# Two transformer blocks on one core: a norm's factors on the weights' rows instead of on the transposed tokens

## The chip, the cores and the metric

One core of one Trainium2 chip runs the whole kernel. The metric is device time in microseconds of one execution. Below, PE is TensorE, DVE is VectorE, ACT is ScalarE, POOL is GpSimd and SP is SyncE; "PEld" is PE's loading of a stationary operand.

## What is computed

The input is 256 tokens of width 1024. A first block of two hybrid layers (retention, sparse attention, a linear recurrence, each ending in a layer norm) is followed by a second block of two layers, all in float32. The second block is where the change is:

```python
def rmsnorm(x, g):
    y = xf * lax.rsqrt(jnp.mean(xf * xf, axis=-1, keepdims=True) + EPS)
    return y * g

def second_block(x, ...):
    h = x
    for i in range(2):
        u = rmsnorm(h, norm_mix[i])
        if i == 0:
            h = h + dsw_mixer(u, a_w_qkv, ...)     # dilated sliding windows
        else:
            h = h + moba_mixer(u, b_w_qkv, ...)    # block attention
        h = h + sq_relu_mlp(rmsnorm(h, norm_ffn[i]), ffn_w1[i], ffn_w2[i])
    return h
```

Each of the four norms has two factors: one per token (the reciprocal root, which the kernel applies after the matrix products) and one per column of the 1024 (`g`, four vectors in all). A product `(x * g) @ W` is the same as `x @ (g[:, None] * W)`, so `g` can go to the tokens or to the rows of the weights.

## The kernel before

Every matrix product in float32 is made of three products of halves. A tensor is split into a high part, rounded to the type float32r, and a low part, the remainder; then `high*high + high*low + low*high` is summed in PSUM (`mm3`, L314 to L316; L415 and L416 in `b_wide`, which makes two of the three in one instruction of 512 columns). The split is one ACT instruction (a copy into float32r, L324) and one DVE instruction (source minus high part, L325), in `split`.

**Weights** lie in DRAM already packed in the order of use, in chunks of two halves. `load_half` gives a half two buffers `wh` and `wl` (eight of each, `W_BUFS`) and a raw buffer `wr` (three, `R_BUFS`), issues one DMA on SP and splits the whole half with one ACT and one DVE instruction. So the raw buffer of the third half back must have been read by DVE before the next DMA is issued, and the `wh` buffer of the eighth half back must have been let go by PE before ACT can write. A half holds 128 rows of the weights in each of several "row blocks" k laid side by side: two blocks of 384 columns for the dilated-window projections (`dq`, `dk`, `dv`; 48 halves), two of 512 for the block-attention projections (`mqk` 16 halves, `mv` 8), four of 256 for the up-projections (`f1`, 64 halves over both layers). Output and down-projections (`do`, `mo`, `f2`) follow no norm.

**Tokens** are kept both plain (`xn`, two tiles of 128 tokens) and transposed and split (`xh`, `xl`: 8 row blocks by 256 tokens). After each sublayer the steps `R{t}.{hf}` (tile t, column half hf) add the sublayer's output to `xn` on DVE (L944, L946; in the hybrid layer the layer norm of L833 and L834) and call `transposed`: four PE transposes into one PSUM bank (L863), then the split into `x`. Where a norm follows, `transposed` multiplies the four row blocks by their factors while it splits them: four ACT instructions with `scale=g[j]` (L870) and four DVE instructions (L872), each 128 columns. Where none follows (between the two hybrid layers, `gi is None`), it calls `split`, one ACT and one DVE instruction of 512 columns. There are four such norms and four calls per norm. The factors lie in `par`, one value per partition, loaded at the start.

**Order of work.** Within a sublayer the steps are issued in an order written by hand in a string (`HYB`, `DSW`, `MOBA`, `FFN`), then the framework orders each engine's queue by simulated times; steps in brackets keep their written order on PE. The end of the second hybrid layer is `... S1 ] R0.0 [ R0.1 R1.1 ] R1.0`: the second tile's upper columns come before its lower ones. The dilated-window stage starts `k0.0 b1 q0.0 k0.1 q0.1 k1.0 v0.0 k1.1 q1.0 q1.1 v0.1 v1.0 ...`, where `k1.0` loads the weights of k1 (four halves) and projects tile 0, and `k1.1` projects tile 1 with the same weights. After a projection of q or k, `head_norm` copies it on ACT (L904), squares it, sums on DVE (L907), takes a power on POOL (L426), scales on DVE, and PE transposes it (L991); the result is split for the scores (L501 and L503 for keys). The feed-forward stage runs `U{c}` (up-projection of chunk c: weights `f1`, product in `b_wide`, L1112 to L1114 and a split of the result) and `D{c}.{t}` (down-projection, weights `f2`); `U{c+3}` is issued behind `D{c}`, and the first chunk (`E`) runs by tiles, so that it can start on tile 0.

The functions that the change touches, as they were:

Of the kernel before, what the change touches and what calls it, by code (L numbers as in the profile page):

```python
# [9 lines left out]
F32 = mybir.dt.float32  # L10
F32R = mybir.dt.float32r
AF = mybir.ActivationFunctionType
OP = mybir.AluOpType
# [62 lines left out]
    return out  # L76


CHUNKS = _chunks()
OFFS, _o = {}, 0  # L80
for _k, (_a, _l, _r, _c) in CHUNKS.items():
# [8 lines left out]
P_POS, P_CW, P_CB, P_BA, P_BX, P_LAM, P_GAIN, P_G = 0, 128, 144, 148, 152, 156, 160, 164  # L90
# [181 lines left out]
def body(ctx, tc, a, out, stop=None):  # L272
    nc = tc.nc
    V, A, T, G = nc.vector, nc.scalar, nc.tensor, nc.gpsimd
    wts = a["wts"]
# [18 lines left out]
    def load_half(key, i, pieces=1):  # L294
        off, nk, n = OFFS[key]
        m = nk // 2 * n
        h = wp.tile([128, 1024], F32R, name="wh", tag="wh", bufs=W_BUFS)
        l = wp.tile([128, 1024], F32R, name="wl", tag="wl", bufs=W_BUFS)
        rt = wp.tile([128, 1024], F32, name="wr", tag="wr", bufs=R_BUFS)
        w = m // pieces  # L300
        for c in range(0, m, w):
            raw = rt[:, c:c + w]
            nc.sync.dma_start(raw, bass.AP(tensor=wts.tensor, offset=wts.offset + off + i * 128 * m + c,
                                           ap=[[m, 128], [1, w]]))
            split(h[:, c:c + w], l[:, c:c + w], raw)
        return h, l
# [15 lines left out]
    def split(h, l, src):  # L322

        A.activation(h, src, AF.Copy)  # L324
        V.tensor_tensor(l, src, h.bitcast(F32), op=OP.subtract)  # L325


    zero = cst.tile([128, 128], mybir.dt.bfloat16, name="zero")
# [177 lines left out]
    kz = [one.tile([128, 2, 2, S], F32R, name=n, tag=n, bufs=1) for n in ("kh", "kl")]  # L506


    def hybrid(l, nxt, before):
        nonlocal xh, xl, xb  # L510
        ys = [new_y() for _ in range(4)]
        qkT = one.tile([128, 4, S], F32, name="qkT", tag="qkT", bufs=1)
# [316 lines left out]
        def norm(t, hf):  # L829

            q = halves[hf]
            nm, rs, sub = mem["norm", t]
            V.scalar_tensor_tensor(xn[t][:, q], xn[t][:, q], nm, gb[0][:, q], op0=sub, op1=OP.mult)  # L833
            V.scalar_tensor_tensor(xn[t][:, q], xn[t][:, q], rs, gb[1][:, q], op0=OP.mult, op1=OP.add)  # L834
            transposed(xT, t, hf, nxt)

        halves = [slice(hf * 512, hf * 512 + 512) for hf in range(2)]
        gb, xT = [], []
# [16 lines left out]
        run(steps, HYB[l])  # L855
        xh, xl, xb = xT

    def transposed(xT, t, hf, gi):

        tp = bank("s", "xtp")  # L860
        for j in range(4):
            c = hf * 512 + j * 128
            T.transpose(tp[:, j * 128:j * 128 + 128], xn[t][:, c:c + 128], ident)  # L863
        h, l = (x[:, 4 * hf:4 * hf + 4, t * 128:t * 128 + 128] for x in xT[:2])
        tv = tp.rearrange("p (j s) -> p j s", j=4)
        if gi is None:
            return split(h, l, tv)
        g = [par[:, P_G + 8 * gi + 4 * hf + j:P_G + 8 * gi + 4 * hf + j + 1] for j in range(4)]
        for j in range(4):
            A.activation(h[:, j], tv[:, j], AF.Copy, scale=g[j])  # L870
        for j in range(4):
            V.scalar_tensor_tensor(l[:, j], tv[:, j], g[j], h[:, j].bitcast(F32), op0=OP.mult, op1=OP.subtract)  # L872

    def rms(name):

# [15 lines left out]
    def new_keys(shape):  # L891

        return [pool.tile(shape, F32R, name=n, tag=n, bufs=2) for n in ("akh", "akl")]

    def scaled_split(h, l, src, g):

        A.activation(h, src, AF.Copy, scale=g)
        V.scalar_tensor_tensor(l, src, g, h.bitcast(F32), op0=OP.mult, op1=OP.subtract)

    def head_norm(src, n, r, r2, name):  # L900

# [30 lines left out]
                             start=i == 0, stop=i == n - 1)  # L932
        return op[:, :256]

    def residual_steps(os_, scale, gi):

        xT = []

        def add(t, hf):
            if gi is not None and not xT:  # L940
                xT.extend(new_xT())
            q = slice(hf * 512, hf * 512 + 512)
            if scale is None:
                V.tensor_tensor(xn[t][:, q], xn[t][:, q], os_[t][hf], op=OP.add)  # L944
            else:
                V.scalar_tensor_tensor(xn[t][:, q], os_[t][hf], scale[t], xn[t][:, q], op0=OP.mult, op1=OP.add)  # L946
            if gi is not None:
                transposed(xT, t, hf, gi)
            else:
                nc.sync.dma_start(out[t * 128:t * 128 + 128, q], xn[t][:, q])  # L950
        return xT, {f"R{t}.{hf}": (lambda t=t, hf=hf: add(t, hf)) for t in range(2) for hf in range(2)}

    def dsw(r, gi):


        nonlocal xh, xl, xb
# [67 lines left out]
        for s in range(4):  # L1024
            steps |= {f"b{s}": lambda s=s: biased(s), f"w{s}": lambda s=s: weighted(s)}
            for t in range(2):
                steps |= {f"{n}{s}.{t}": lambda n=n, s=s, t=t: proj(n, s, t) for n in "qkv"}
                steps[f"a{s}.{t}"] = lambda s=s, t=t: attend(s, t)
        xT, more = residual_steps(os_, None, gi)
        run(steps | more, DSW)  # L1030
        if xT:
            xh, xl, xb = xT

    def moba(r, gi):
        nonlocal xh, xl, xb
        r2 = squares(r, "r2")
        ys = [new_y() for _ in range(4)]
        mem = {}

        def biased(s):  # L1040
            mem["b", s] = bias = pool.tile([128, 4, 256], F32, name="mbias", tag="bias", bufs=2)
            nc.sync.dma_start(bias, a["mb"][s].rearrange("p (n w) -> p n w", w=256))

        def proj(s, t):
            if t == 0:
                mem["w", s] = [load(("mqk", s, j)) for j in (0, 1)]
                mem["q", s] = new_q()
                mem["k", s] = new_keys([128, 2, 2, S])
            o = bank("acc", "mqk")
            a_proj(mem["w", s], o, t)  # L1050
            x = head_norm(o, 8, r[t], r2[t], "m")
            tp = bank("t", "mtp")
            for j in range(4):
                T.transpose(tp[:, j * 128:j * 128 + 128], x[:, j * 128:j * 128 + 128], ident)
            tv = tp.rearrange("p (j s) -> p j s", j=4)
            q = slice(t * 128, t * 128 + 128)
            scaled_split(*(x[:, :2, q] for x in mem["q", s]), tv[:, 0:2], gains[:, 1:2])
            halves_split(*([x[:, :, hd, q] for hd in range(2)] for x in mem["k", s]), tv[:, 2:4])

        def mv(s):  # L1060
            v = mem["v", s] = pool.tile([128, 2, 512], F32, name="mv", tag="v", bufs=V_BUFS)
            c = [load(("mv", s, j)) for j in (0, 1)]
            for t in range(2):
                o = bank("acc", "mv")
                a_proj(c, o, t)
                A.activation(v[:, t], o, AF.Copy, scale=r[t])

        def attend(s, p, t):
            bias, (qh, ql), k, v = (mem[x, s // 2 * 2 if x == "v" else s] for x in "bqkv")
            n = 128 * (t + 1)  # L1070
            c = 256 * (s % 2) + 128 * p
            q = slice(t * 128, t * 128 + 128)
            sc = bank("s", "as")
            mm3(sc[:, :2 * n].rearrange("p (h n) -> p h n", h=2), qh[:, p, q], ql[:, p, q],
                *(x[:, p, :, :n] for x in k), True, True)
            pt = softmax_unit([[(sc[:, n * hd:n * hd + n], bias[:, 2 * p + hd, 256 - n:])] for hd in range(2)], n)
            mem["pt", s, p, t] = [[(v[:, j, c + 64 * hd:c + 64 * hd + 64],
                                    pt[:, hd * n + j * 128:hd * n + j * 128 + 128]) for j in range(t + 1)]
                                  for hd in range(2)]

        def weighted(s, p):
            op = values([mem.pop(("pt", s, p, t)) for t in range(2)])
            split(ys[s][0][:, p], ys[s][1][:, p], op)
        os_, steps = out_steps([("mo", j) for j in range(4)], ys)
        for s in range(4):
            steps[f"b{s}"] = lambda s=s: biased(s)
            if s % 2 == 0:
                steps[f"v{s}"] = lambda s=s: mv(s)
            for t in range(2):
                steps[f"q{s}.{t}"] = lambda s=s, t=t: proj(s, t)  # L1090
                for p in range(2):
                    steps[f"a{s}.{p}.{t}"] = lambda s=s, p=p, t=t: attend(s, p, t)
                    steps[f"w{s}.{p}"] = lambda s=s, p=p: weighted(s, p)
        xT, more = residual_steps(os_, None, gi)
        run(steps | more, MOBA)
        if xT:
            xh, xl, xb = xT

    def ffn(i, gi):
        nonlocal xh, xl, xb  # L1100
        os_ = accumulators()
        hid, w2 = {}, {}
# [49 lines left out]
                V.tensor_tensor(q, x, x, op=OP.mult)  # L1152
                r2.append(q)
        r2 = []
        xT, steps = residual_steps(os_, r2, gi)
        steps |= {"E": lambda: up_early(EARLY), "r": norms}
        steps |= {f"U{c}": lambda c=c: up(c) for c in range(16) if c not in EARLY}
        steps |= {f"D{c}.{t}": lambda c=c, t=t: down_step(c, t) for c in range(16) for t in range(2)}
# [10 lines left out]
            behind(xn[t], src)  # L1169
            nc.sync.dma_start(xn[t], a["xn"][t])  # L1170

    hybrid(0, None, load_x)
    if stop == 1:
        return dump()
    hybrid(1, 0, None)
    if stop == 2:
        return dump()
    ctx1.close()
    pool = ctx.enter_context(tc.tile_pool(name="block2", bufs=1, reuse_waits="tile"))
    dsw(rms("r"), 1 if stop != 3 else None)  # L1180
    if stop == 3:
        return
    ffn(0, 2 if stop != 4 else None)
    if stop == 4:
        return
    moba(rms("r"), 3 if stop != 5 else None)
    if stop == 5:
        return
    ffn(1, None)


def build(arrays, stop=None):
# [19 lines left out]
```

## Time and profile before

| | us |
|---|---|
| runs | 929.26, 930.4, 933.69 (median 930.4) |
| the profiled execution, its own time | 932.65 |
| its span, first to last instruction | 930.9 |
| PE busy | 906.0 (97%) |
| PE loading weights | 786.3 (84%) |
| DVE busy | 659.3 (71%) |
| ACT busy | 533.9 (57%) |
| DMA | 155.22 MB, mean 167 GB/s |

The stages by time: the first hybrid layer to about 154 us, the second to 305, dilated windows to 450, the first feed-forward stage to 629, block attention to 747, the second feed-forward stage to the end. A matmul's busy time covers its pipelined end, so that PE's 97% is not PE at its peak; what counts is where PE has no instruction at all. In a timeline row, the bracket at the end gives the idle time before an instruction on its engine and what ended it. In groups, "x48" is a count, and the column behind the bar is busy time and the mean of one in ns.

### The profile page before, as it was taken

What the parts mean: (1) busy time and instruction counts of PE and PEld (TensorE: products, weight loads), DVE (VectorE), ACT (ScalarE), POOL (GpSimd) and SP (SyncE); (2) the same over time, 40 slices, a digit from 0 to 9 for tenths busy, and PEclk for the clock granted to TensorE, in tenths of its full rate; (3) what the DMA queues carried; (4) which work ended last, traced back from release to release, by engine and by line L of the source; (5) the groups of instructions that cost most, each with busy time, mean ns of one, the idle gap of its engine ahead of it and who ended that gap; (6) DMA issues with size and microseconds to landing.
All of it is one profiled execution on the core that took longest, in us unless ns stands there. A gap on an engine that the chain in (4) does not pass through costs nothing.

```text
span 930.9 us, 14698 instructions
## 1 busy us (share of the span) xinstructions
PE 906.0 (97%) x5430; PEld 786.3 (84%) x5430; DVE 659.3 (71%) x1426; ACT 533.9 (57%) x1002; POOL 55.3 (6%) x59
## 2 busy tenths in 40 slices
PE   8999998999999999999999999999999999999998
PEld 6998876988978889997888888888887788888886
DVE  5778957678868788787766666658888576665662
ACT  5456852545764677776754554457777574445540
POOL 0000000000001321120000000002111000000000
PEclk9999998999999999999999999999999999999999
DMA  7765333663325446654455565655654176566551
GB/s 239 236 232 166 113 124 108 204 204 116 118 80 171 154 140 191 205 158 155 143 180 195 195 193 183 188 172 181 185 175 139 46 226 190 194 194 190 182 159 46
DMA packets 45721, 155.22 MB, mean 167 GB/s; under 512 B 5072, under 2 KB 5456, under 8 KB 45648
## 3 DMA queue, kind: packets, MB, share of 16 engines
q1 hardware_dynamic: 45648, 154.27, 52.1%
q8 instruction: 43, 0.70, 0.3%
q14 instruction: 30, 0.25, 0.1%
HBM read 153.20 MB, written 1.05 MB: 166 GB/s over the span
## 4 chain that ended last, share of the span: by engine, by line
PE 82%; DVE 8%; ACT 5%; DMA 3%; issue 1%; POOL 0%; SPq 0%; DVEq 0%; ACTq 0%
PE f L415 12%; PE o L314 8%; PE o L316 8%; PE o L315 8%; PE f L416 6%; DVE wl L325 3%; DMA wr<-in_wts 3%; PE atp L493 2%; ACT wh L324 2%; PE mqk L315 2%; PE mqk L316 2%; PE mqk L314 2%; PE aop L931 1%; PE as L314 1%; PE as L316 1%
## 5 line engine op out<-in xcount | busy, mean ns | idle before, releaser
L325 DVE TENSOR_TENSOR wl<-wr,wh 128x1024 fp32r<-128x1024 f32 (+3 forms) x285 | 327.0, 1160 | 134.7 <-ACT wh L324 132.5
L324 ACT ACTIVATE wh<-wr 128x1024 fp32r<-128x1024 f32 (+3 forms) x285 | 283.8, 1009 | 158.8 <-DMA wr<-in_wts 61.3
L415 PE MATMUL f<-x,wh 128*128 128x512 f32 x480 | 170.7, 398 | 0.0
L314 PE MATMUL o<-wh,yh 128*128 128x512 f32 x368 | 145.2, 395 | 2.3 <-ACT yh L324 1.5
L315 PE MATMUL o<-wl,yh 128*128 128x512 f32 x368 | 143.7, 391 | 0.0
L316 PE MATMUL o<-wh,yl 128*128 128x512 f32 x368 | 142.7, 392 | 0.0
L416 PE MATMUL f<-x,wl 128*128 128x256 f32 x480 | 134.9, 281 | 0.0
L415 PEld LDWEIGHTS f<-x,wh 128*128 128x128 f32 x480 | 90.2, 188 | 21.6
L416 PEld LDWEIGHTS f<-x,wl 128*128 128x128 f32 x480 | 90.6, 189 | 1.1
L314 PEld LDWEIGHTS o<-wh,yh 128*128 128x128 f32 x368 | 69.1, 188 | 18.3 <-ACT yh L324 2.4
L316 PEld LDWEIGHTS o<-wh,yl 128*128 128x128 f32 x368 | 68.9, 188 | 15.0 <-issue 0.5
L315 PEld LDWEIGHTS o<-wl,yh 128*128 128x128 f32 x368 | 69.1, 188 | 12.8
L484 ACT ACTIVATE pr<-pr,anm 128x256 f32<-128x256 f32 (+2 forms) x112 | 54.0, 486 | 7.8 <-DVE anm L481 7.6
L324 ACT ACTIVATE yh<-fz 128x512 fp32r<-128x512 f32 x30 | 19.0, 632 | 57.5 <-DVE fz L1114 57.4
L1112 ACT ACTIVATE fz<-f 128x256 f32<-128x256 f32 x60 | 22.4, 373 | 41.9 <-PE f L416 41.9
L494 ACT ACTIVATE pt<-atp 128x512 f32<-128x512 f32 (+1 forms) x56 | 31.2, 562 | 19.9 <-PE atp L493 19.6
L325 DVE TENSOR_TENSOR yl<-fz,yh 128x512 fp32r<-128x512 f32 x30 | 20.8, 692 | 19.9 <-ACT yh L324 19.9
L493 PE MATMUL atp<-ident,pr 128*128 128x128 f32 x208 | 33.5, 275 | 1.0 <-DVE akl L503 0.4
L1113 DVE TENSOR_TENSOR fz<-fz,f 128x256 f32<-128x256 f32 x60 | 25.0, 417 | 13.2 <-ACT fz L1112 13.2
L489 DVE TENSOR_SCALAR pr<-pr,adn 128x256 f32<-128x256 f32 (+2 forms) x112 | 33.0, 340 | 1.0
L493 PEld LDWEIGHTS atp<-ident,pr 128*128 128x128 f32 x208 | 25.1, 140 | 6.0 <-issue 0.7
L426 POOL TENSOR_TENSOR dms<-dms,nhalf 128x6 f32<-128x6 f32 x16 | 24.2, 1516 | 88.1 <-DVE dms L908 88.1
(311 smaller groups left out, 1849.6 us busy)
## 6 DMA issues: line engine op xcount, KB each, us to landing
wr<-in_wts SPq DMA_DIRECT2D x227, 512.0 KB, 4.1
wr<-in_wts SPq DMA_DIRECT2D x48, 384.0 KB, 3.5
bias<-in_db SPq DMA_DIRECT2D x4, 640.0 KB, 4.9
wr<-in_wts SPq DMA_DIRECT2D x8, 280.0 KB, 3.0
cw<-in_cw SPq DMA_DIRECT2D x4, 512.0 KB, 4.5
mbias<-in_mb SPq DMA_DIRECT2D x4, 512.0 KB, 3.6
xT<-in_xT SPq DMA_DIRECT2D x4, 256.0 KB, 6.5
lngb<-in_lng SPq DMA_DIRECT2D x2, 512.0 KB, 4.1
```

Of the source, the lines that this page charges most:

```text
L314: T.matmul(o, sh, mh, start=start, stop=False)
L315: T.matmul(o, sh, ml, start=False, stop=False)
L316: T.matmul(o, sl, mh, start=False, stop=stop)
L324: A.activation(h, src, AF.Copy)
L325: V.tensor_tensor(l, src, h.bitcast(F32), op=OP.subtract)
L415: T.matmul(o, c.h(k)[:, q], xb[:, k], start=k == 0, stop=False)
L416: T.matmul(o[:, 0], c.l(k)[:, q], xh[:, k], start=False, stop=k == 7)
L484: A.activation(pr[:, g], pr[:, g], AF.Exp, scale=-1.0, bias=nm[:, i:i + 1], accum_out=dn[:, i:i + 1])
L489: V.tensor_scalar(pr[:, g], pr[:, g], dn[:, i:i + 1], None, op0=OP.mult)
L493: T.transpose(tp[:, j:j + 128], pr[:, j:j + 128], ident)
L494: A.activation(pt[:, :c], tp[:, :c], AF.Copy)
L1113: V.tensor_tensor(zj, zj, o[:, 0], op=OP.add)
```

## The change

The factors leave `transposed`, which now always calls `split` on the whole 512 columns. They go into `load_half`: for a chunk whose input is normed, the half is split in one piece per row block, each by an ACT instruction with `scale` and a DVE instruction with the factor as one value per partition. The DMA of such a half is the same. `scaled_split` existed before, for the queries. The argument that named the norm (`nxt`, `gi`) becomes a flag that says whether this is the last sublayer.

```diff
+GAINS = {"dq": 0, "dk": 0, "dv": 0, "mqk": 2, "mv": 2, "f1": (1, 3)}
...
         rt = wp.tile([128, 1024], F32, name="wr", tag="wr", bufs=R_BUFS)
+        g = GAINS.get(key[0])
+        if g is not None:
+            g = P_G + 8 * (g[key[1]] if key[0] == "f1" else g)
+            nc.sync.dma_start(rt[:, :m], bass.AP(tensor=wts.tensor, offset=wts.offset + off + i * 128 * m,
+                                                 ap=[[m, 128], [1, m]]))
+            for k, row in enumerate(CHUNKS[key][2][i * nk // 2:(i + 1) * nk // 2]):
+                c = slice(k * n, k * n + n)
+                scaled_split(h[:, c], l[:, c], rt[:, c], par[:, g + row:g + row + 1])
+            return h, l
...
+    def scaled_split(h, l, src, g):
+        A.activation(h, src, AF.Copy, scale=g)
+        V.scalar_tensor_tensor(l, src, g, h.bitcast(F32), op0=OP.mult, op1=OP.subtract)
...
-    def transposed(xT, t, hf, gi):
+    def transposed(xT, t, hf):
...
-        if gi is None:
-            return split(h, l, tv)
-        g = [par[:, P_G + 8 * gi + 4 * hf + j:P_G + 8 * gi + 4 * hf + j + 1] for j in range(4)]
-        for j in range(4):
-            A.activation(h[:, j], tv[:, j], AF.Copy, scale=g[j])
-        for j in range(4):
-            V.scalar_tensor_tensor(l[:, j], tv[:, j], g[j], h[:, j].bitcast(F32), op0=OP.mult, op1=OP.subtract)
+        split(h, l, tv)
...
-    def residual_steps(os_, scale, gi):
+    def residual_steps(os_, scale, last):
...
-    dsw(rms("r"), 1 if stop != 3 else None)
+    dsw(rms("r"), stop == 3)
...
-    ffn(0, 2 if stop != 4 else None)
+    ffn(0, stop == 4)
...
-    moba(rms("r"), 3 if stop != 5 else None)
+    moba(rms("r"), stop == 5)
...
-    ffn(1, None)
+    ffn(1, True)
```

## Rows read from the trace of the kernel before

**Rows 1.** Windows by stage: length, busy time of each engine (instructions), PE clock, DMA share, GB/s

```profile
305.00:450.00 145.00, 140.91 (x908) 131.21 (x908) 115.15 (x278) 102.76 (x204) 23.70 (x16) 1.00 0.53 162
...
450.00:629.00 179.00, 178.43 (x921) 151.89 (x922) 113.95 (x151) 91.85 (x135) 1.64 (x3) 1.00 0.58 184
...
629.00:747.00 118.00, 116.83 (x633) 94.61 (x631) 91.12 (x240) 83.07 (x188) 16.45 (x9) 1.00 0.48 148
...
sum 931.00, PE 905.96 PEld 786.26 DVE 659.33 ACT 533.90 POOL 55.29; mean PE 150.99 PEld 131.04 DVE 109.89 ACT 88.98 POOL 9.22
```

**Rows 2.** Chain that ended last, shares of the span by engine

```profile
PE 82%; DVE 8%; ACT 5%; DMA 3%; issue 1%; POOL 0%; SPq 0%; DVEq 0%; ACTq 0%
```

**Rows 3.** Groups by form, the split of a weight half: busy us, mean ns, idle before, releasers

```profile
L325 DVE TENSOR_TENSOR wl<-wr,wh 128x1024 fp32r<-128x1024 f32 x227 | 274.4, 1222 | 123.2 <-ACT wh L324 121.6
...
L324 ACT ACTIVATE wh<-wr 128x1024 fp32r<-128x1024 f32 x227 | 237.0, 1058 | 128.2 <-DMA wr<-in_wts 44.8 <-PE f L415 34.0 <-PE o L316 32.6
...
L325 DVE TENSOR_TENSOR wl<-wr,wh 128x768 fp32r<-128x768 f32 x48 | 45.5, 955 | 10.3 <-ACT wh L324 9.6
...
L324 ACT ACTIVATE wh<-wr 128x768 fp32r<-128x768 f32 x48 | 40.2, 847 | 22.5 <-DMA wr<-in_wts 9.4 <-PE o L316 6.8 <-PE dk L316 2.4
```

**Rows 4.** Groups by form, the nearest rows for the new pieces and the old ones

```profile
L757 DVE SCALAR_TENSOR_TENSOR xc<-lxp,par,xc 128x256 f32<-128x256 f32 x12 | 5.3, 478 | 0.0
...
L834 DVE SCALAR_TENSOR_TENSOR xn<-xn,lrs,lngb 128x512 f32<-128x512 f32 x8 | 5.7, 745 | 0.0
...
L484 ACT ACTIVATE pr<-pr,anm 128x256 f32<-128x256 f32 x48 | 23.9, 501 | 5.8 <-DVE anm L481 5.6
...
L484 ACT ACTIVATE pr<-pr,anm 128x512 f32<-128x512 f32 x16 | 11.4, 715 | 1.8 <-DVE anm L481 1.8
...
L870 ACT ACTIVATE x<-xtp,par 128x128 fp32r<-128x128 f32 x64 | 17.9, 385 | 3.3 <-PE xtp L863 3.2
...
L872 DVE SCALAR_TENSOR_TENSOR x<-xtp,par,x 128x128 fp32r<-128x128 f32 x64 | 17.6, 342 | 1.7 <-ACT x L870 1.7
...
L494 ACT ACTIVATE pt<-atp 128x512 f32<-128x512 f32 x48 | 28.2, 594 | 17.0 <-PE atp L493 16.7
...
L944 DVE TENSOR_TENSOR xn<-xn,o 128x512 f32<-128x512 f32 x8 | 5.4, 683 | 2.0 <-PE o L316 2.0
```

**Rows 5.** Timeline: start us, us, instruction; runs of one instruction in a queue

```profile
298.53 1.41 DVE L833 SCALAR_TENSOR_TENSOR xn<-xn,lmv,lngb 128x512 f32<-128x512 f32 x2
...
303.69 2.17 ACT L870 ACTIVATE x<-xtp,par 128x128 fp32r<-128x128 f32 x8
```

**Rows 6.** Timeline of PE into the dilated-window stage: idle before, and what ended it

```profile
293.08 0.44 PE L314 MATMUL dk<-wh,x 128*128 128x384 f32 x1 [0.72 <-ACT x L870]
...
294.98 0.44 PE L316 MATMUL dk<-wh,x 128*128 128x384 f32 x1 [0.94 <-DVE x L872]
...
305.14 0.45 PE L314 MATMUL dk<-wh,x 128*128 128x384 f32 x1 [1.37 <-ACT x L870]
```

**Rows 7.** Timeline of PE at 329 us, and the group by form of dv's matmuls

```profile
329.32 0.52 PE L991 MATMUL dtp<-ident,qn 128*128 128x128 f32 x3 [0.64 <-DVE akl L503]
...
L314 PE MATMUL dv<-wh,x 128*128 128x384 f32 x64 | 21.7, 339 | 0.0
```

**Rows 8.** Chain of waits in order of time, the tail of the dilated-window stage

```profile
422.69 0.94 ACT wh L324
...
424.34 0.95 ACT wh L324
```

**Rows 9.** Timeline of PE into the two feed-forward stages

```profile
450.10 0.66 PE L863 MATMUL xtp<-ident,xn 128*128 128x128 f32 x4 [1.07 <-DVE xn L944]
...
747.57 0.66 PE L863 MATMUL xtp<-ident,xn 128*128 128x128 f32 x4 [0.61 <-DVE xn L944]
```

**Rows 10.** Between the two layers of block one: timeline of PE, and windows

```profile
153.54 0.80 PE L316 MATMUL A1o<-wh,x 128*128 128x512 f32 x1 [1.88 <-DVE x L325]
...
150.00:160.00 10.00, 7.46 (x20) 5.76 (x21) 6.40 (x12) 0.60 (x1) 0.98 (x1) 0.66 0.32 109
```

More of the change, by code (lines that the diff above doesn't have):

```diff
@@ L506, in body, with hybrid @@
     kz = [one.tile([128, 2, 2, S], F32R, name=n, tag=n, bufs=1) for n in ("kh", "kl")]
-    def hybrid(l, nxt, before):
+    def hybrid(l, before):
         nonlocal xh, xl, xb
@@ L834, in norm @@
             V.scalar_tensor_tensor(xn[t][:, q], xn[t][:, q], rs, gb[1][:, q], op0=OP.mult, op1=OP.add)
-            transposed(xT, t, hf, nxt)
+            transposed(xT, t, hf)
         halves = [slice(hf * 512, hf * 512 + 512) for hf in range(2)]
@@ L893, in new_keys @@
         return [pool.tile(shape, F32R, name=n, tag=n, bufs=2) for n in ("akh", "akl")]
-    def scaled_split(h, l, src, g):
-        A.activation(h, src, AF.Copy, scale=g)
-        V.scalar_tensor_tensor(l, src, g, h.bitcast(F32), op0=OP.mult, op1=OP.subtract)
     def head_norm(src, n, r, r2, name):
@@ L933, in values @@
         return op[:, :256]
-    def residual_steps(os_, scale, gi):
+    def residual_steps(os_, scale, last):
         xT = []
         def add(t, hf):
-            if gi is not None and not xT:
+            if not last and not xT:
                 xT.extend(new_xT())
@@ L946, in add @@
                 V.scalar_tensor_tensor(xn[t][:, q], os_[t][hf], scale[t], xn[t][:, q], op0=OP.mult, op1=OP.add)
-            if gi is not None:
-                transposed(xT, t, hf, gi)
+            if not last:
+                transposed(xT, t, hf)
             else:
@@ L951, in residual_steps, with dsw @@
         return xT, {f"R{t}.{hf}": (lambda t=t, hf=hf: add(t, hf)) for t in range(2) for hf in range(2)}
-    def dsw(r, gi):
+    def dsw(r, last):
         nonlocal xh, xl, xb
@@ L1028, in dsw @@
                 steps[f"a{s}.{t}"] = lambda s=s, t=t: attend(s, t)
-        xT, more = residual_steps(os_, None, gi)
+        xT, more = residual_steps(os_, None, last)
         run(steps | more, DSW)
@@ L1032, in dsw, with moba @@
             xh, xl, xb = xT
-    def moba(r, gi):
+    def moba(r, last):
         nonlocal xh, xl, xb
@@ L1093, in moba @@
                     steps[f"w{s}.{p}"] = lambda s=s, p=p: weighted(s, p)
-        xT, more = residual_steps(os_, None, gi)
+        xT, more = residual_steps(os_, None, last)
         run(steps | more, MOBA)
@@ L1097, in moba, with ffn @@
             xh, xl, xb = xT
-    def ffn(i, gi):
+    def ffn(i, last):
         nonlocal xh, xl, xb
@@ L1154, in ffn @@
         r2 = []
-        xT, steps = residual_steps(os_, r2, gi)
+        xT, steps = residual_steps(os_, r2, last)
         steps |= {"E": lambda: up_early(EARLY), "r": norms}
@@ L1170, in load_x @@
             nc.sync.dma_start(xn[t], a["xn"][t])
-    hybrid(0, None, load_x)
+    hybrid(0, load_x)
     if stop == 1:
         return dump()
-    hybrid(1, 0, None)
+    hybrid(1, None)
     if stop == 2:
```

## Prediction

> **What bounds the kernel now.** I read the sums by stage first, then the chain of waits, then the groups by form, and last the timelines around the gaps of PE. The sums say that PE is busy 905.96 of 931 us, DVE 659.33, ACT 533.90 [rows 1]. The chain that ended last is PE for 82%, DVE for 8%, ACT for 5% [rows 2]. So PE's own work is the time, and DVE and ACT matter only where PE stands still for them: 25 us in all. The change adds no work to PE and takes none away, so it is worth what it does to those gaps, and what new ones it opens.
>
> The three stages shown have different covers. In the first feed-forward stage (450 to 629 us) PE is busy 178.43 of 179 us, with DVE at 64% and ACT at 51%. In the dilated-window stage (305 to 450) PE idles 4.1 of 145 us, with DVE at 79% and ACT at 71%. In the block-attention stage (629 to 747) PE idles 1.2 of 118 us, with DVE at 77% and ACT at 70% [rows 1]. The dilated-window stage has the least room.
>
> **What one instruction costs.** A weight half of 1024 columns takes ACT 1058 ns and DVE 1222 ns, one of 768 columns 847 and 955 ns [rows 3]. These have no factor. The nearest rows with one value per partition as a factor, out of SBUF: DVE 478 ns for 256 columns (L757) and 745 for 512 (L834); ACT 501 ns for 256 and 715 for 512, an Exp that also sums (L484) [rows 4]. For 384 I take the middle, 611 and 608 ns. Instructions in a queue overlap: two L833, of L834's form, take 1.41 us together, 0.08 less; eight L870 of 385 ns take 2.17 us, so each after the first adds 0.255 and overlaps by 0.13 [rows 4, 5]. I take 0.08 off each DVE instruction and 0.12 off each ACT one and count in such slots:
> - a half of an up-projection (f1), now four pieces of 256: DVE 4 x 0.40 = 1.59 for 1.14 (+0.45 us), ACT 4 x 0.38 = 1.52 for 0.94 (+0.58);
> - a half of the dilated-window projections (dq, dk, dv), two pieces of 384: DVE 2 x 0.53 = 1.06 for 0.875 (+0.19), ACT 2 x 0.49 = 0.98 for 0.73 (+0.25);
> - a half of mqk or mv, two pieces of 512: DVE 2 x 0.665 = 1.33 for 1.14 (+0.19), ACT 2 x 0.595 = 1.19 for 0.94 (+0.25);
> - a transposed quarter of the tokens, sixteen times: DVE 4 x 0.26 = 1.05 becomes one of about 683 ns (L944, same size, one side in PSUM), 0.60 (-0.45); ACT 4 x 0.255 = 1.02 becomes one of about 594 ns (L494, the same size out of PSUM), 0.47 (-0.55).
>
> There are 64 f1 halves, 48 of the second kind (the x48 of the 768-column rows) and 24 of the third. DVE: 28.8 + 9.1 + 4.6 - 7.2 = +35 us. ACT: 37.1 + 12.0 + 6.0 - 8.8 = +46 us. The lower bound for ACT is that the factor costs nothing: L494 without one takes 594 ns where L484 with one takes 715 [rows 4], 0.12 less a piece, some +12 us in all.
>
> The sum goes by these rows. [...]
>
> **Where the added time lies.** DMA issues stay as they are, one per half on SP. POOL gets nothing.
>
> *Feed-forward stages: 0.* Per pair of chunks, 179 / 16 = 11.2 us, two f1 halves add 0.9 to DVE's 7.1 and 1.2 to ACT's 5.7 [rows 1]. The cover: eight weight buffers, four used per 11.2 us, so a buffer is refilled some 16 to 20 us before PE reads it again; ACT's largest wait there is for PE to let go of a buffer (L415, 34.0 us) [rows 3]. The up-projection's own results are made about two chunks before they are used. If that cover were gone, the price would be 32 x 0.58 = 19 us per stage; nothing in the rows points there.
>
> *Last norm of block one into the dilated-window stage: +0.65.* PE stands 0.72 us for the first ACT piece of the transposed tokens, 0.94 for the first DVE piece and 1.37 for ACT again [rows 6]. With one wide instruction PE no longer gets its first row block after 0.385 us but after 0.594: +0.21, and the weight half queued ahead on ACT is 0.25 longer: +0.46. On DVE 0.683 for 0.342, and +0.19 for the half ahead: +0.53. The third gap is different: the second token tile does columns 512 up first (R1.1 before R1.0), so PE waits for the fifth of eight pieces, 4 x 0.255 + 0.385 = 1.41 us after they start at 303.69 [rows 5]; now it is the second of two, 0.47 + 0.594 = 1.07: -0.34. The upper end for the second gap is the nearest row of the wide form itself: between the two layers of block one the tokens are already split in one piece, without a factor, and there PE stood 1.88 us for DVE [rows 10], 0.94 more than now instead of 0.53. The lower end is that all three gaps go, -3.0.
>
> *Head of the dilated-window stage: +1.0.* Before PE's gap at 329 us (0.64 for the DVE split of a key [rows 7]) the ten halves of k1, v0 and the start of q1 are split: 10 x 0.19 = 1.9 on DVE, 2.5 on ACT, ahead of the head norms this gap waits for. DVE is free a fifth of the stage, so some of it is absorbed; I take half of 1.9, with 0 and 2.5 as ends. Behind a DVE piece that waits for its ACT piece stand those norms, and for them PE's transposes.
>
> *Its tail: +1.2.* Two f1 halves for the next stage are split by ACT between the exponentials; both stand in the chain of waits (422.69 and 424.34) [rows 8]. 2 x 0.58; the ends are 0, if ACT's queue is planned otherwise, and 1.2.
>
> *Into the feed-forward stages: 0 and +0.3.* PE waits 1.07 and 0.61 us for the residual sums on DVE [rows 9], which stand behind weight splits. In the first, two f1 halves (+0.9 at most) meet shorter token pieces (-0.45 each): 0, ends -0.5 and +0.9. In the second, ACT's and DVE's pieces run side by side, so one half is done as early as before, and only the next, queued on ACT, is later by 0.58 less a wait of about 0.3: +0.3, ends -0.6 and +1.2.
>
> *Block-attention stage: 0.* 24 halves add 4.6 to DVE, which is free 27 of 118 us [rows 1]. Upper end: that PE's idle 1.2 doubles.
>
> **Sum:** 0.65 + 1.0 + 1.2 + 0 + 0.3 = +3.15 us. The profiled execution took 932.65 us (span 930.9), which gives 935.8; it stands 2.25 above the median of the runs, 930.4, so the forecast is 933.5 us, +0.3%. 0.5%, 4.7 us, is about what a measurement of this kernel can tell from no change.
>
> **Rivals.** *Faster:* PE is held up by DVE's and ACT's lateness, not by their load, and shorter queues at the norms plus finer weight pieces end that. All gaps that wait for tokens or residual sums go: 0.72 + 0.94 + 1.37 + 1.07 + 0.61 = 4.7 us, and the 0.64 at 329: 925 us. For it: the chain runs through DVE at these places. Against: weight splits, which grow, stand ahead of every one of them. [...]
>
> *Slower:* in the dilated-window stage the splits become what PE waits for. With 40 halves and four of f1, DVE comes to about 124 of 145 us and ACT to 115. It decides from the point where a half is split later than PE wants it: today the matmuls of dv never wait [rows 7]. If they do from k1 to k2, 20 halves in series, it costs 20 x 0.25 = 5.0 instead of 1.0, and with the tail's 1.2, 0.65, and the upper ends 0.9 and 1.2 the sum is 8.95: 939.4 us. [...]
>
> *No effect on the chain:* every term is absorbed, 930 to 931 us. I count it with the forecast.
>
> **How the numbers follow.** Forecast with its absorbed form 0.48, most of it inside 0.5%, a little beyond where the clock falls once; slower 0.35; faster 0.17, of which a part stays inside 0.5%. Order on the engines is planned over simulated times, so a gap may also move to another place; that widens the sides, and more on the slower one, since load grows. From these: faster by over 0.5% 0.15, within 0.44, slower 0.41. The range: low from the faster case less its last gaps, 927; high between the slower case without and with the clock, 942. Both signs hold much, so the likeliest case alone: 930 to 937.
>
> **What would show it.** Right: in the changed profile x4 groups of f1 at about 480 to 510 ns; DVE near 695 and ACT near 580 us busy; PE's busy time within 1 us; feed-forward without gaps; new idle time of PE in 290 to 345 and 420 to 455 us. Wrong: PE gaps that name wh or wl in the dilated-window stage (slower rival), gaps at x and xn gone (faster), or PE's busy time itself changed.

## The result and the profile after

The changed kernel takes 935.3 us (median of 15 runs, 932.64 to 938.39), the kernel before 930.05 in 15 runs (928.17 to 933.94). The ratio is 1.0051, 95% interval [1.0038, 1.0064]: slower by half a per cent, inside the forecast range and 1.8 us above the forecast. Against the kernel before in the same 15 runs the change is +5.25 us, where +3.15 was forecast. The profiled execution took 936.4 us, its span is 934.5 (before 930.9), the mean granted clock 0.992 (before 0.993).

Windows by stage after (columns as in [rows 1]):

```profile
305.00:450.00 145.00, 140.97 (x912) 131.80 (x911) 122.32 (x326) 113.82 (x252) 23.50 (x16) 1.00 0.53 163
450.00:629.00 179.00, 178.34 (x919) 151.90 (x920) 124.00 (x225) 107.16 (x211) 1.64 (x3) 1.00 0.59 185
629.00:747.00 118.00, 114.45 (x620) 92.57 (x619) 90.93 (x249) 85.89 (x201) 15.00 (x9) 1.00 0.46 143
```

DVE rose from 659.3 to 689.7 us, ACT from 533.9 to 581.5, PE stayed at 906.5. The dilated-window stage carries 7 us more on DVE and 11 more on ACT, the feed-forward stage 10 and 15, and in both PE is as busy as before. The stage that lost is block attention: in the same 118 us PE did 114.45 us of work for 116.83, although DVE is no busier there and ACT only by 2.8 us.

Groups by form after, for the new pieces and the tokens' split (L342 and L341 are `scaled_split`, L337 is the DVE half of `split`):

```profile
L342 DVE SCALAR_TENSOR_TENSOR wl<-wr,par,wh 128x256 fp32r<-128x256 f32 x256 | 109.3, 481 | 30.7 <-ACT wh L341 30.4
L341 ACT ACTIVATE wh<-wr,par 128x256 fp32r<-128x256 f32 x256 | 109.1, 498 | 32.9 <-PE f L432 23.9 <-PE o L328 4.7 <-DMA wr<-in_wts 1.7
...
L342 DVE SCALAR_TENSOR_TENSOR wl<-wr,par,wh 128x384 fp32r<-128x384 f32 x96 | 55.9, 612 | 9.1 <-ACT wh L341 8.8
L341 ACT ACTIVATE wh<-wr,par 128x384 fp32r<-128x384 f32 x96 | 53.3, 609 | 16.5 <-DMA wr<-in_wts 6.2 <-PE o L328 5.7 <-PE dk L328 3.5
L342 DVE SCALAR_TENSOR_TENSOR wl<-wr,par,wh 128x512 fp32r<-128x512 f32 x48 | 34.3, 746 | 4.1 <-ACT wh L341 3.8
L341 ACT ACTIVATE wh<-wr,par 128x512 fp32r<-128x512 f32 x48 | 31.5, 716 | 4.6 <-DMA wr<-in_wts 1.5 <-PE o L328 1.0 <-PE f L432 1.0
...
L337 DVE TENSOR_TENSOR x<-xtp,x 128x512 fp32r<-128x512 f32 x20 | 13.3, 681 | 0.7 <-ACT x L336 0.7
```

These are the instructions as the prediction priced them. Where the time went is in PE's gaps. First the timeline of PE before, the gaps that [rows 6, 7, 9] did not show; then the timeline of PE after (the bracket is the idle time before the instruction and what ended it):

```profile
306.43 0.45 PE L316 MATMUL dk<-wh,x 128*128 128x384 f32 x1 [0.31 <-DVE x L872]
...
330.61 0.45 PE L314 MATMUL dq<-wh,x 128*128 128x384 f32 x1 [0.77 <-ACT qn L904]
...
425.81 0.50 PE L314 MATMUL o<-wh,yh 128*128 128x512 f32 x1 [0.28 <-ACT dv L987]
...
717.13 0.50 PE L314 MATMUL as<-akh,aqh 128*128 128x256 f32 x2 [0.70 <-ACT akh L501]
...
718.50 0.44 PE L493 MATMUL atp<-ident,pr 128*128 128x128 f32 x2 [0.43 <-DVE akl L503]
```

```profile
292.71 0.44 PE L326 MATMUL dk<-wh,x 128*128 128x384 f32 x1 [1.03 <-ACT x L336]
294.24 0.44 PE L328 MATMUL dk<-wh,x 128*128 128x384 f32 x1 [0.55 <-DVE x L337]
304.71 0.44 PE L326 MATMUL dk<-wh,x 128*128 128x384 f32 x1 [1.68 <-ACT x L336]
328.06 0.44 PE L326 MATMUL dq<-wh,x 128*128 128x384 f32 x1 [0.39 <-ACT qn L910]
425.60 0.50 PE L326 MATMUL o<-wh,yh 128*128 128x512 f32 x1 [2.09 <-ACT dv L993]
450.65 0.38 PE L326 MATMUL f<-wh,x 128*128 128x256 f32 x1 [1.08 <-DVE x L337]
715.72 0.38 PE L326 MATMUL as<-akh,aqh 128*128 128x256 f32 x1 [1.04 <-ACT akh L518]
721.81 0.50 PE L326 MATMUL o<-wh,yh 128*128 128x512 f32 x1 [0.97 <-ACT yh L336]
734.07 0.33 PE L937 MATMUL aop<-pt,mv 128*64 128x128 f32 x2 [0.94 <-DVE yl L337]
750.45 0.33 PE L880 MATMUL xtp<-ident,xn 128*128 128x128 f32 x1 [0.78 <-DVE xn L950]
755.09 0.39 PE L326 MATMUL f<-wh,x 128*128 128x256 f32 x1 [0.52 <-DVE x L337]
```

By place, with the gaps too small to show added (0.47 for `x` at the first feed-forward before; after, 0.22 for `xn` there, and 0.34 and 0.25 in block attention):

| place | PE idle before | after | difference | forecast |
|---|---|---|---|---|
| into the dilated-window stage | 3.34 | 3.26 | -0.08 | +0.65 |
| its head | 1.41 | 0.39 | -1.02 | +1.0 |
| its tail | 0.28 | 2.09 | +1.81 | +1.2 |
| into the first feed-forward | 1.54 | 1.30 | -0.24 | 0 |
| end of block attention | 1.13 | 3.54 | +2.41 | 0 |
| into the second feed-forward | 0.61 | 1.30 | +0.69 | +0.3 |
| sum | 8.31 | 11.88 | +3.57 | +3.15 |

The spans of this pair of profiles differ by 3.66 us, about what these gaps add up to. The medians differ by 5.25: the profile of before was one of its slower executions (932.65 us, 2.6 above the median), so some 1.6 us of the loss lie outside what this pair can show. The largest term is one that the forecast had at 0, and the one at the head has the wrong sign.

The lengths of the stretches between PE's first matmuls of `dk`, of the first `f`, of `mqk` and of the second `f` say the same without a choice of gaps. From before to after they change by -0.4 us (start to `dk`), -0.2 (`dk` to `f`), +0.1 (`f` to `mqk`), +3.4 (`mqk` to `f`, 118.4 to 121.7) and +0.8 (from there to the end). So block attention with its way into the second feed-forward is nearly the whole loss of this pair.

The gaps at the end of block attention come from other work: `akh`, `yh` and `yl` after, `akh` and `akl` before. PE's own order had changed. In the programs as built, 855 of PE's 5106 instructions stand at another place than before, all of them between the start of the dilated-window stage and the second feed-forward. That is the framework's doing: it orders the queues by simulated times, and the change alters those. The runs below therefore exchange orders and loads.

### The profile page after: what moved, and what is told of

Same layout as the page of the kernel before. It is cut to its first block, busy times and chain, and to the rows that moved or that the text cites. A ratio compares the mean times of both kernels' runs of the same rounds, so it can differ in the third digit from the quotient of the medians.

```text
span 934.5 us, 15126 instructions
## 1 busy us (share of the span) xinstructions
PE 906.5 (97%) x5430; PEld 786.4 (84%) x5430; DVE 689.7 (74%) x1642; ACT 581.5 (62%) x1218; POOL 54.0 (6%) x59
## 4 chain that ended last, share of the span: by engine, by line
PE 80%; DVE 9%; ACT 5%; DMA 4%; issue 2%; SPq 0%; ACTq 0%; DVEq 0%
PE f L432 12%; PE o L326 8%; PE o L328 8%; PE o L327 8%; PE f L433 6%; DMA wr<-in_wts 4%; DVE wl L337 2%; PE atp L510 2%; PE mqk L327 2%; PE mqk L328 2%; PE mqk L326 2%; PE aop L937 2%; ACT wh L336 1%; PE as L326 1%; PE as L328 1%
## 5 line engine op out<-in xcount | busy, mean ns | idle before, releaser
L337 DVE TENSOR_TENSOR wl<-wr,wh 128x1024 fp32r<-128x1024 f32 (+2 forms) x149 | 174.1, 1189 | 80.6 <-ACT wh L336 79.6
L342 DVE SCALAR_TENSOR_TENSOR wl<-wr,par,wh 128x256 fp32r<-128x256 f32 (+2 forms) x400 | 199.6, 545 | 44.0 <-ACT wh L341 43.0
L341 ACT ACTIVATE wh<-wr,par 128x256 fp32r<-128x256 f32 (+2 forms) x400 | 193.9, 551 | 54.0 <-PE f L432 24.8
L336 ACT ACTIVATE wh<-wr 128x1024 fp32r<-128x1024 f32 (+2 forms) x149 | 150.4, 1029 | 100.1 <-DMA wr<-in_wts 43.4
```

## The experiments

Two questions: which of the four norms costs what, and whether a cost is the load (longer splits) or the plan (another order of the queues).

**One norm at a time.** The factors of one norm go to the rows of the weights, those of the others stay on the tokens; `ON` is `(0,)` for the dilated-window projections, `(1,)` for the first up-projection, `(2,)` for block attention, `(3,)` for the second up-projection.

```diff
+ON = (0,)
...
+        if g in ON:
+            g = P_G + 8 * g
...
-        if gi is None:
+        if gi is None or gi in ON:
             return split(h, l, tv)
```

*only_norm0.* Expected: 

> The change for the first norm alone: factors on the rows of dq, dk and dv, plain wide split of the tokens into the dilated-window stage; the other three norms as before. Theory A (the terms of the prediction, each at its place): 0.65 + 1.0 = +1.6 us. Theory B (the loss is one place, the end of the block attention, where the up-projection's first halves are split while the last heads are worked on): 0 to -0.5 us here. Theory C (the loss follows the added work of DVE and ACT, 42.5 us of DVE before savings, wherever it lies): 9.1 / 42.5 of 4.75 = +1.0 us.

*only_norm1.* Expected: 

> The change for the second norm alone: factors on the rows of f1 of the first feed-forward layer. Theory A: the tail of the dilated-window stage, +1.2 us. Theory B: 0. Theory C: 14.4 / 42.5 of 4.75 = +1.6 us.

*only_norm2.* Expected: 

> The change for the third norm alone: factors on the rows of mqk and mv. Theory A: 0. Theory B: 0 to +1, since the block attention's own splits grow a little (0.19 us of DVE a half, 24 halves), but they are over before its last 40 us. Theory C: 4.6 / 42.5 of 4.75 = +0.5 us.

*only_norm3.* Expected: 

> The change for the fourth norm alone: factors on the rows of f1 of the second feed-forward layer. Theory A: +0.3 us. Theory B: nearly the whole loss, +3.5 to +4.5 us, with PE gaps of some 2.5 us more between the last query projection and the first up-projection. Theory C: 14.4 / 42.5 of 4.75 = +1.6 us.

Measured, against 35 runs of the kernel before on the same chip (median 930.33):

| | median us | ratio, 95% interval | mean granted clock | sum of PE's gaps at its places, before and with it |
|---|---|---|---|---|
| only_norm0 | 928.32 | 0.9983 [0.9968, 0.9998] | 0.9939 | 5.03, 3.19 |
| only_norm1 | 932.42 | 1.0033 [1.0015, 1.0050] | 0.9922 | 0.28, 2.22 (tail) |
| only_norm2 | 932.95 | 1.0032 [1.0018, 1.0047] | 0.9937 | 1.74, 4.09 |
| only_norm3 | 931.90 | 1.0024 [1.0007, 1.0040] | 0.9927 | 0.61, 1.32 |
| before | 930.33 | | 0.9938 | |

The four add to +0.72%; each is known to about 0.15%, so they agree with the 0.51% of the whole. The gaps of one profile each do not cover every loss: they make 2.35 of the 3.0 us of only_norm2, 1.94 of the 3.1 of only_norm1 and 0.71 of the 2.2 of only_norm3. All three theories fall: the first has the wrong sign at norm 0 and nothing at norm 2, the second puts the loss on norm 3, and by the third norm 0 would have lost. PE's order differs from before's in 451, 40, 308 and 56 places, which are the 855 of the whole change. In the traces the first differences of norms 1 and 3 come behind their gaps (from 430 and 753 us on, on before's time axis), so at those gaps PE's order is that of before; norms 0 and 2 re-order PE in the stages that their factors enter.

The timeline of PE with norm 0 alone: the head's 1.41 is 0.39, as with the whole change, and the tail's gap does not grow (0.15):

```profile
291.85 0.45 PE L327 MATMUL dk<-wh,x 128*128 128x384 f32 x1 [1.00 <-ACT x L337]
293.41 0.44 PE L329 MATMUL dk<-wh,x 128*128 128x384 f32 x1 [0.59 <-DVE x L338]
303.24 0.44 PE L327 MATMUL dk<-wh,x 128*128 128x384 f32 x1 [1.06 <-ACT x L337]
326.61 0.45 PE L327 MATMUL dq<-wh,x 128*128 128x384 f32 x1 [0.39 <-ACT qn L917]
```

The timelines of ACT before (its first `f1` half at this place; the other two are those of [rows 8]), and then of ACT and PE with norm 1 alone, at the end of the dilated-window stage:

```profile
420.62 1.06 ACT L324 ACTIVATE wh<-wr 128x1024 fp32r<-128x1024 f32 x1
```

```profile
416.96 1.70 ACT L910 ACTIVATE wh<-wr,par 128x256 fp32r<-128x256 f32 x4
...
419.58 0.50 ACT L910 ACTIVATE wh<-wr,par 128x256 fp32r<-128x256 f32 x1
...
420.68 2.90 ACT L910 ACTIVATE wh<-wr,par 128x256 fp32r<-128x256 f32 x7
423.48 0.57 ACT L1000 ACTIVATE dv<-dv,rp 128x384 f32<-128x384 f32 x1
...
424.10 0.50 PE L327 MATMUL o<-wh,yh 128*128 128x512 f32 x1 [2.22 <-ACT dv L1000]
```

Seven pieces of `f1` (2.90 us, 0.40 apart) stand in ACT's queue right ahead of the last `dv`, for which PE waits 2.22 us. From the first of the three halves to `dv` ACT takes 6.52 us (416.96 to 423.48) where before it took 4.57 (420.62 to 425.19); the 1.95 more is the growth of the gap. The tail is what the prediction said, ACT's queue, and larger.

The timeline of PE with norm 2 alone, at the end of block attention, has the gaps of the whole change:

```profile
714.32 0.50 PE L327 MATMUL as<-akh,aqh 128*128 128x256 f32 x2 [1.30 <-ACT akh L514]
720.14 0.50 PE L327 MATMUL o<-wh,yh 128*128 128x512 f32 x1 [0.97 <-ACT yh L337]
...
732.41 0.88 PE L944 MATMUL aop<-pt,mv 128*64 128x128 f32 x12 [0.94 <-DVE yl L338]
```

The weights of norm 2 (`mqk`, `mv`) are all split before these gaps, the last by 682.6 us on DVE, and none of the gaps names a weight. So the question is the plan.

**The order exchanged.** PE's queue is tied to a given order, one instruction behind the other, and all else is planned as usual: the changed kernel and norm 2 alone in the order of before, and the kernel before in the order of after.

```diff
+def pinned(tc):
+    made = [i for i in tc.nc.cur_bb.bb.instructions if i.engine == tc.nc.tensor.engine]
...
+    info = mybir.DependencyInfo(mybir.DependencyClass.NoSync, mybir.DependencyReason.DATA)
+    for x, y in zip(order, order[1:]):
+        tc.add_manual_dep(made[y], made[x].name, info, reason="PE order")
...
+    pinned(tc)
```

*after_old_order.* Expected: 

> All of the change's instructions, with TensorE held to the order of the matmuls and transposes that it had before the change (the other engines' orders are still planned anew). Theory D, the planned order: the loss comes from the re-planned order of the matmuls, so with the old one the time is within 1 us of the kernel before (ratio 0.999 to 1.001), and the 2 to 5 us between the last query projection and the second feed-forward are back to 39 us from 43.5. Theory E, the load: the loss comes from the time of the added pieces on VectorE and ScalarE, whatever the order, so the ratio stays at 1.004 to 1.006, with gaps of other lengths at the same stages.

*before_new_order.* Expected: 

> None of the change's instructions: the kernel before, with TensorE held to the order that the change gave it. Theory D, the planned order: it loses as the change does, 3 to 5 us (ratio 1.003 to 1.005). Theory E, the load: within 1 us of the kernel before (0.999 to 1.001). Should both this run and the one with the old order lose, each order fits only its own loads, and neither theory stands alone.

*norm2_old_order.* Expected: 

> The factors of block two's first norm alone on the rows of the weights, as in only_norm2, with TensorE held to the order before the change. only_norm2 measured 1.0032, with 43.3 us from the last query projection to the second feed-forward against 39.2 before. Theory D, the planned order: 0.999 to 1.001 and about 39 to 40 us there. Theory E, the load: 1.002 to 1.004 and 42 us or more there.

Measured against 26 runs of before (median 930.33): before_new_order 934.07 us, ratio 1.0046 [1.0031, 1.0060]; norm2_old_order 930.94, 1.0006 [0.9993, 1.0018]; after_old_order 932.59, 1.0014 [0.9997, 1.0031]. The whole change in the old order stands between the two theories, nearer to D. With norm 2 it is the plan: with the old order its loss is gone (within 0.2%), and without one instruction of the change the new order gives the gaps (before_new_order holds the new order of all four norms). The stretch from `mqk` to the second `f` shows it too: 118.4 us before, 121.5 in only_norm2, 121.3 in before_new_order, 118.3 in norm2_old_order. The timelines of PE at the end of block attention, of before_new_order and of norm2_old_order:

```profile
714.99 0.50 PE L345 MATMUL as<-akh,aqh 128*128 128x256 f32 x2 [1.26 <-ACT akh L532]
720.86 0.50 PE L345 MATMUL o<-wh,yh 128*128 128x512 f32 x1 [0.97 <-ACT yh L355]
...
733.12 0.88 PE L962 MATMUL aop<-pt,mv 128*64 128x128 f32 x12 [0.94 <-DVE yl L356]
```

```profile
716.26 0.50 PE L358 MATMUL as<-akh,aqh 128*128 128x256 f32 x2 [0.71 <-ACT akh L545]
717.63 0.44 PE L537 MATMUL atp<-ident,pr 128*128 128x128 f32 x2 [0.43 <-DVE akl L547]
```

The first, with two smaller ones (0.12 and 0.25), add up to 3.54 us as in the changed kernel, the second are those of the kernel before, to 0.01 us. What the order does can be read there: before, 28 instructions, six of them matmuls of `o`, stand between the twelve `aop` that start at 712.13 us and the scores `as` that wait for `akh`, and PE waits 0.70. In the new order the six come ahead of the `aop`, two transposes are left between these and the scores, and PE waits 1.26.

before_new_order also has a gap of only 0.39 at the head, but this does not show a gain by the order. PE's clock had a mean of 0.83 over 300 to 310 us there, where before it was 1.00, and PE took as long from `dk` to here as before (37.5 us, below): it came to the gap later and waited less. only_norm1 shows the same with neither the order nor the load of before changed up to that place. Its window and its timeline of PE:

```profile
300.00:310.00 10.00, 8.28 (x39) 7.68 (x38) 7.74 (x21) 6.07 (x15) 3.19 (x3) 0.83 0.16 58
...
326.98 0.44 PE L327 MATMUL dq<-wh,x 128*128 128x384 f32 x1 [0.33 <-ACT qn L917]
```

From the first matmul of `dk` to that of `dq` behind this gap, PE takes 37.5 us before, 37.5 in before_new_order and 37.4 in only_norm1, but 35.4 in the changed kernel and 35.1 in after_old_order (clock 1.00 there in both). So what is gained at the head comes with the change's instructions, in the old order of PE as well; whether the new order alone would gain at a full clock is open.

after_old_order keeps a remainder, and its profile shows where. Timeline of PE, and the window of the first of these rows (the clock is the third column from the end):

```profile
425.93 0.61 PE L357 MATMUL o<-wh,yh 128*128 128x512 f32 x1 [2.22 <-ACT dv L1024]
...
749.35 0.33 PE L911 MATMUL xtp<-ident,xn 128*128 128x128 f32 x1 [1.02 <-DVE xn L981]
...
754.04 0.38 PE L357 MATMUL f<-wh,x 128*128 128x256 f32 x1 [0.57 <-DVE x L368]
...
420.00:430.00 10.00, 7.78 (x35) 6.45 (x35) 8.54 (x23) 8.56 (x23) 0.00 (x0) 0.83 0.71 212
```

The tail's 2.22 us is there in the old order of PE too; here the clock fell with it (a mean of 0.83 over these 10 us; an estimate from that mean is up to 1.7 us of PE's work). What is left are norms 1 and 3.

**Norm 1 taken apart, and two versions in a fixed order.** `norm1_wide_tokens` leaves the factors of this norm out: its tokens are split by the quarter, the halves of `f1` whole. `norm1_plain_pieces` keeps the factors on the tokens and splits `f1` in pieces without one. The other two put norms 0 and 2, and norms 0, 2 and 3, on the weights, with PE in the order of only_norm0 (that of before from the end of the dilated-window stage on).

```diff
 # norm1_wide_tokens, against before
-        if gi is None:
+        if gi is None or gi in ON:
             return split(h, l, tv)
 # norm1_plain_pieces, against only_norm1
-                scaled_split(h[:, c], l[:, c], rt[:, c], par[:, g + row:g + row + 1])
+                split(h[:, c], l[:, c], rt[:, c])
...
-        if gi is None or gi in ON:
+        if gi is None:
 # norms02_fixed_order, norms023_fixed_order, against only_norm0
-ON = (0,)
+ON = (0, 2)
...
+    pinned(tc)
```

*norm1_wide_tokens.* Expected: 

> Only the gain half of the change at the first feed-forward: its tokens are split by the quarter without their factors, and the halves of f1 stay whole; the factors of this norm are left out of the result. only_norm1 measured 1.0033, with 2.22 us of idle TensorE at 421.88 us, behind a dv that ScalarE splits after eleven pieces of f1. TensorE's order is that of before. Theory F, the pieces on ScalarE: without them that gap is back to 0.28 us or less, and the ratio is 0.998 to 1.000. Theory G, the wide tokens or the order: a gap of 1 us or more stays before the first feed-forward, and the ratio is 1.002 to 1.004.

*norm1_plain_pieces.* Expected: 

> Only the loss half of the change at the first feed-forward: the halves of f1 are split in four pieces of 256 columns, without a factor, and the tokens keep theirs. Theory F, the pieces on ScalarE: a plain piece costs less than the 498 ns of one with a factor (some 400), so four take 1.6 us a half on ScalarE against 1.06 whole; dv's split is still late at the end of the dilated-window stage, by 1 to 2 us, and the ratio is 1.001 to 1.003. Theory G: under 0.5 us of gap there, ratio 0.999 to 1.001.

*norms02_fixed_order.* Expected: 

> The factors of both blocks' first norms on the rows of the weights (norms 0 and 2), and those of the feed-forwards' norms left on the tokens; TensorE is held to the order of only_norm0, which in block attention is that of before. only_norm0 measured 0.9983. Theory D, the planned order: norm 2 is free with the old order, so the ratio is 0.997 to 0.999. Theory E, the load: norm 2's pieces cost their 2 to 3 us all the same, ratio 1.000 to 1.002.

*norms023_fixed_order.* Expected: 

> As norms02_fixed_order, with the second feed-forward's norm (3) on the rows of f1 too; TensorE in the same order. only_norm3 measured 1.0024 with its own order. Theory D, the planned order: norm 3 is free as well, 0.997 to 0.999. Theory E, the load: 1.5 us over norms02_fixed_order, of which 0.5 to 1 us is a gap at the second feed-forward's start.

Measured against 35 runs of before (median 930.72): norm1_wide_tokens 929.48 us, 0.9998 [0.9984, 1.0013]; norm1_plain_pieces 931.59, 1.0014 [0.9998, 1.0029]; norms02_fixed_order 928.13, 0.9979 [0.9966, 0.9992]; norms023_fixed_order 930.2, 1.0001 [0.9988, 1.0014]. PE's wait for `dv` at the tail, wide tokens first, then plain pieces:

```profile
426.70 0.50 PE L315 MATMUL o<-wh,yh 128*128 128x512 f32 x1 [0.27 <-ACT dv L988]
```

```profile
427.71 0.50 PE L327 MATMUL o<-wh,yh 128*128 128x512 f32 x1 [1.11 <-ACT dv L1000]
```

0.27 whole, 1.11 in plain pieces, 2.22 in pieces with a factor. ACT's time from the first `f1` half to `dv` is 4.56, 5.40 and 6.52 us in these three, so the gap grows by what ACT's queue grows; the ratio goes the same way (0.9998, 1.0014, 1.0033), though neighbouring intervals overlap. Theory F holds for norm 1: it is ACT's load ahead of `dv`. Norm 2 is free in a fixed order, as theory D had it: norms 0 and 2 together are at 0.9979, so this version is 0.2% faster than the kernel before, with an interval that leaves 1 out. It cannot be told from norm 0 alone (0.9983).

Norm 3 is not free in a fixed order. It adds 2.1 us to norms02_fixed_order; the timeline of PE in norms023_fixed_order shows 0.95 of it (the first gap was 0.72 without norm 3, the second 0):

```profile
743.57 0.33 PE L907 MATMUL xtp<-ident,xn 128*128 128x128 f32 x1 [0.93 <-DVE xn L988]
...
748.43 0.39 PE L358 MATMUL f<-wh,x 128*128 128x256 f32 x1 [0.74 <-DVE x L369]
```

**Norm 3's tokens alone**, as `norm1_wide_tokens` with `ON = (3,)`; the factors of this norm are left out.

*norm3_wide_tokens.* Expected: 

> Only the gain half of the change at the second feed-forward: its tokens are split by the quarter without their factors, and the halves of f1 stay whole; the factors of this norm are left out of the result. only_norm3 measured 1.0024, with a gap of 0.52 us before the first f, in which TensorE waits for the tokens' low half that VectorE splits late; norms023_fixed_order has the same gap (0.74 us) in the other order. Theory H, the wide tokens are late by themselves: a gap of 0.4 us or more is left there, ratio 1.001 to 1.003. Theory F, the pieces of f1 on VectorE and ScalarE hold the tokens up: no gap over 0.2 us by the tokens' low half there, ratio 0.998 to 1.001.

Measured 933.1 us against 930.26 (17 runs of before): 1.0026 [1.0008, 1.0045], the loss of only_norm3 without one piece of `f1`. But the gap is not the one that either theory named. Timelines of DVE and PE, and then of DVE before:

```profile
743.01 0.68 DVE L945 TENSOR_TENSOR xn<-xn,o 128x512 f32<-128x512 f32 x1
744.45 1.23 DVE L326 TENSOR_TENSOR wl<-wr,wh 128x1024 fp32r<-128x1024 f32 x1 [0.75 <-ACT wh L325]
745.59 0.68 DVE L945 TENSOR_TENSOR xn<-xn,o 128x512 f32<-128x512 f32 x1
...
746.33 0.72 PE L864 MATMUL xtp<-ident,xn 128*128 128x128 f32 x4 [1.92 <-DVE xn L945]
```

```profile
745.69 1.22 DVE L325 TENSOR_TENSOR wl<-wr,wh 128x1024 fp32r<-128x1024 f32 x1 [1.03 <-ACT wh L324]
746.83 1.28 DVE L944 TENSOR_TENSOR xn<-xn,o 128x512 f32<-128x512 f32 x2
```

Before, the two residual sums stand together behind a weight split. Here the split stands between them, DVE waits 0.75 us for ACT, splits for 1.23, and PE's second set of transposes waits 1.92. So here a lighter load lost as much as the heavier one, through the order of DVE's queue; PE's order up to there is that of before. In this profile the clock fell there too (0.84 over 740 to 750 us, 1.00 before); an estimate from that mean is up to 1.6 us of PE's work, so it can be part of the loss. This is the reading of one profile; whether norm 3 would be free with DVE's and ACT's queues held too was not tried.

## Why the prediction was right, and where its steps were not

The total was inside the range, and the ratio lies on the line between "within 0.5%" and slower, which had 0.44 and 0.41. That the total came so near was luck: by the table the terms are off by -0.73, -2.02, +0.61, -0.24, +2.41 and +0.39 us, which cancel to +0.42. Measured by the medians the change was 2.1 us larger than forecast. The sentence that 0.5% is about what can be told from no change was too cautious: the interval is 0.13% to either side. Of the five signs of being right four came; the fifth only in part, since the new idle time lies in 420 to 455 us and PE idled less, not more, in 290 to 345.

**What one instruction costs: right.** 481, 612 and 746 ns on DVE against 478, 611 and 745; 498, 609 and 716 on ACT against 501, 608 and 715. A slot is 0.40 us on both engines (seven in 2.90 us on ACT, six in 2.48 on DVE) against 0.40 and 0.38. The sums came to +30.4 us on DVE and +47.6 on ACT, for +35 and +46. The lower bound of +12 for ACT does not follow from its own figures: 0.12 less on each of the 400 pieces is 48 us, more than the whole +46. Plain pieces measured 0.09 less.

**Feed-forward stages, 0: right** in their interior. In the first one 10 us more on DVE and 15 on ACT left PE's 178.3 busy of 179 us as they were. That the buffers ahead were the cover is the prediction's account; no run takes them away.

**Tail of the dilated-window stage, +1.2: right in cause, too small.** It counted the two halves of [rows 8] at 0.58; a third, at 420.62 us, is not in the chain of waits. ACT split twelve pieces of `f1`, three halves, between 416.96 and `dv` at 423.48 us (the expectations said eleven), seven of them in a row just ahead of it; three halves give 1.74, and the gap grew by 1.81 (1.94 with norm 1 alone). The clock may come on top: only_norm1's runs have a mean granted clock of 0.9922 against 0.9938, but the difference is only about twice its standard error.

**Into the dilated-window stage, +0.65, and its head, +1.0: wrong, the second in sign.** The 0.94 fell to 0.55 where +0.53 was expected, and the 1.37 rose to 1.68 where -0.34 was. At the head the step "I take half of 1.9, with 0 and 2.5 as ends" kept the queue as it was and allowed no gain; PE's 0.64 and 0.77 became one gap of 0.39. It is 0.30 in after_old_order, so PE's order is not needed for the gain. Which of the change's instructions on DVE and ACT give it, the wide tokens or the pieces, stays open.

**Block attention, 0 with an upper end of 1.2: the step that failed.** DVE's free 27 of 118 us did cover the 24 halves, as norm2_old_order shows (1.0006). But a share of free time says nothing of a re-planned queue: +2.41 us of gaps, +3.4 over the stretch from `mqk` to the second `f`. The sentence that a gap may "move to another place", because the order is planned, stood among the chances and should have been a term of the sum.

**Into the second feed-forward, +0.3: right in sign, less than half of what came.** It measured 0.69, and by norm3_wide_tokens an order can give such a gap, here that of DVE's queue.

**The rivals.** No gap of the dilated-window stage after names `wh` or `wl`, so the slower rival did not happen. The upper end of the range, 942, also counts a fall of the clock in that case, and no run shows this term. What the profiles show of the clock is this. The changed kernel has a granted clock of 1.00 over 290 to 310 us, behind gaps of 1.03, 0.55 and 1.68 us. Five other profiles have 0.83 over 290 to 300 us (an estimate from that mean is up to 1.7 us of PE's work), with gaps of 0.50 to 1.09 us; in only_norm2 they were 0.75 and 0.90, much as before, where the clock was 1.00. And behind the gap of 1.88 us of [rows 10] the kernel before has 0.50 from 152.6 to 159.3 us, with matmuls of 512 columns 0.43 us apart, where 0.23 follow at 1.00 from 160 us on. The faster one holds for norm 0 alone: -1.84 us of gaps, 0.9983. Its finer weight pieces went the other way at norm 1: the pieces, even without a factor, took PE's wait from 0.27 to 1.11 us (norm1_wide_tokens, norm1_plain_pieces).

## What to carry to other kernels

Where a framework plans the queues, a change to a few instructions is two changes: their load, and a new order of all that is planned with them. Compare the orders first, and run the old kernel in the new order and the new one in the old before explaining a gap by load. Put the factor where no finer-grained work waits on the same queue: for the projections of a mixer it cost nothing or gained, with PE's order held (norms 0 and 2: 0.9979); for the first up-projection it delayed the stage that ran beside its weights' splits (norm 1: PE's wait of 0.28 us became 2.22).

## What was not expected of the hardware

The factor as such has a price on both engines: a plain piece of 256 columns took 408 ns on ACT and 419 on DVE (norm1_plain_pieces), one with a factor 498 and 481 (on DVE the one with a factor is also another operation, SCALAR_TENSOR_TENSOR). And equal gaps did not have equal consequences for the clock: behind 2.22 us of idle PE at the tail the profile of after_old_order shows 0.83 over 420 to 430 us, the one of only_norm1, with the same 2.22 us, 1.00. The mean granted clock goes with much of the spread between runs of one kernel: before took 927.87 us at a mean granted clock of 0.998 and 934.33 at 0.990. These two ends give 0.8 us for each 0.001, a straight line through all 35 runs 0.6 (correlation -0.75). By the line, an estimate, the clock would be 1.0 of the 3.1 us that only_norm1 lost, beside its gap's 1.94; the two mean clocks are too close for more than that.
